# Second layer of a two-layer decoder: Gram masks, a pair's norm, key transposes and exponentials issued at other places

## The chip, the cores and the metric

The kernel runs on one core of one Trainium2 chip, as one program. The metric is the device time of one execution in microseconds; the median of three runs is compared. Five engines work beside each other, each through a queue of its own in the order that was fixed when the program was built: TensorE (PE in the profile; PEld is its loading of weights), VectorE (DVE), ScalarE (ACT), GpSimd (POOL) and SyncE (SP), which issues most of the transfers. An instruction that waits holds everything behind it in its queue.

## The reference, cut to what matters

Two residual layers work on 512 tokens of width 2048, in float32. The first is gated differential attention and isn't touched. The second is RWKV-7 time mixing with 32 heads of 64 channels:

```python
p = h @ w_in
p = p + (token_shift(p) - p) * mu
r, k, v, g, dw, da = jnp.split(p, RW_SPLITS, axis=-1)
w_log = -jax.nn.softplus(-(w0 + jnp.tanh(dw) @ decay_up)) - 0.5
decay = jnp.exp(-jnp.exp(w_log))
a = jax.nn.sigmoid(a0 + da @ iclr_up)
kk = heads(k * k_k)
kk = kk / jnp.maximum(jnp.sqrt(jnp.sum(kk * kk, axis=-1, keepdims=True)), 1e-12)
k = k * (1.0 + (a - 1.0) * k_a)
# wkv7_scan(r, decay, k, v, -kk, kk * a), for each token:
sa = jnp.einsum('bhvk,bhk->bhv', S, a_t)
S = S * w_t[:, :, None, :] + sa[..., None] * b_t[:, :, None, :] + v_t[..., None] * k_t[:, :, None, :]
y = jnp.einsum('bhvk,bhk->bhv', S, r_t)
# then
y = (y - mean) * lax.rsqrt(var + GN_EPS)
y = y * gn_w + gn_b + jnp.sum(r * k * r_k, axis=-1, keepdims=True) * v
x = x + (y * jax.nn.silu(g)) @ w_out
```

## The kernel before, in words

**Pairs.** The second layer goes through 16 pairs of heads (`j` from 0 to 15; 128 channels each). The 512 tokens lie in 8 chunks of 64. For a pair, four projections of the width 128 are computed one after the other: V of pair `j` (`proj(2, j)`), K of pair `j+1` (`begin(j + 1)`), the gate of pair `j-3` (from `j` = 3 on; `proj(3, j - LAG)`) and the receptance of pair `j+1` (`receptances(j + 1)`). Each is 48 matmuls of 128x512 (L129, into `pp`): 16 blocks of the contraction by three products of high and low parts, because float32 values are split in two parts. The weights of a projection are loaded in two halves, and for each half ACT makes two tiles of high parts (`wh`, L115) and DVE two of low parts (`wl`, L116).

**Positions.** Every projection matmul is a tick. What follows calls V18 the place behind the 18th matmul of V, and so K, g (gate) and r (receptance). `behind=[(at, f)]` calls `f` behind the matmul `at`. Two trains of small work advance on ticks: the scan of pair `j-1` (class `Chain`, `scan_pair`) and the triangular solve of pair `j` (class `Solve`, `t_solve`).

**The scan.** In a full pair (`j` from 3 to 14) it starts at V3, and the gaps between its steps are 7, 7 and 8 ticks. A chunk c has three steps: the matmul L1322 and the copy of its result to `rhs` (ACT, L1325); the matmul L1333 and the copy to `VS` (ACT, L1335); the matmul L1340 and the state for the next chunk, `VS` from DVE (L1344; L1347 for chunk 0). So L1322 of chunk c is at tick 3 + 22c, L1340 at 17 + 22c: L1340 of chunk 1 at V39, of chunk 4 at tick 105 of the pair (g9), of chunk 5 at 127 (g31), of chunk 6 at 149 (r5). POOL copies the state to `SA` (L1328) and scales it (`Sg`, L1331). `others` is work that goes behind the state of a given chunk: `turn_keys` (four transposes into the PSUM tag `pb`, L1171, and the copy to `BKT`, L1172) at chunks 0 and 1, that is at V17 and V39, `turn_values` at 4, `finish_y` at 5. After chunk 7 come `outputs` (L1362, L1366) and `centre` (`yc`, L1377 to L1379).

**The Gram matrices.** `gram` stands at V18: 32 matmuls (L1123), the first half into the two buffers of `pb`, the second into those of `pc`; ACT copies them to `G` (L1127) and to `LP` (L1132). Behind that, `mask_gram` sets triangles of `G` to zero on POOL (L1158, L1160; four instructions for a pair). The masked parts are read by the next pair's scan and its outputs. Then `t_solve`: 12 ticks on, at V30, the transpose `LT` (DVE, L1189), the bound and the reciprocal of the squared norms `n2` (L1195, L1196), then 31 steps of two DVE instructions (L1200, L1203), 3 or 4 ticks apart; they end at tick 138 of a full pair (g42), and there follow the product with `n2` (L1205) and the transposes `T1` (L1207) and `W` (L1210). `t_first` (L1230; r9) and `t_second` (L1245; r33) join the halves of the inverse.

**The norms.** `norms` (r24) sums the squares of the keys by two matmuls (L1043, L1044; `pt<-sHx,ones` and `pt<-sLx,ones`), copies them to `ssl` (L1144), and sends them through DRAM with three transfers from POOL's queue (L1148 twice, L1151) to lie as `n2`.

**Keys of the next pair.** `stage1` leaves three parts in `g.later`: `decays` (a scan on DVE, L1073, then the exponentials on ACT, L1077 to L1079, and `f`, L1080), `queries` (DVE, then the scales of `BK` on ACT, L1087) and `keys` (DVE product L1091, squares L1093, their split L916 and L917). One of them is traced behind each new state, so in a full pair behind chunks 4, 5 and 6. What is left over is traced at the head of `norms` or of `stage2`.

**The group norm** of a pair (`group_norm`: square `ysq` on ACT, L1387; sums L1389; an inverse root of eleven small DVE instructions, L63 to L70; the product L1393) is called at V18 of the pair after next.

**What sets the order.** The program is traced first, and a planner then gives each engine its order: of what is ready by its own reckoning it takes what has the highest priority. A priority falls with the place in the trace, `high_priority(offset)` raises it (scan 5000, solve 4000, weight splits 2000). So work that is ready early can be issued far ahead of its place. `issue_after(ins)` puts what a block traces behind `ins` on the same engine's queue; `behind(g, ins)` (the function, L1175) puts an instruction of any engine behind the matmul of the current tick, as an order for the planner with no wait at run time. Tiles of a tag share its buffers: `thg` has one buffer for the gate's `th`, `k2`, `ssl` and `ysq`, and a tile waits until the one before has been read.

Of the kernel before, what the change touches and what calls it, by code (L numbers as in the profile page):

```python
# [18 lines left out]
ALU = mybir.AluOpType  # L19
# [4 lines left out]
P = 128  # L24
D = 2048
# [927 lines left out]
C = 64  # L953
NC_ = T // C
HALF = 32
NG = 4
# [71 lines left out]
LAG = 3  # L1028
# [15 lines left out]
    g.nc.tensor.matmul(out, ones, l[:], start=False, stop=True)  # L1044


def stage1(g, j, k, up):


    nc, w = g.nc, g.work  # L1050
    p = Pair()
    col = lambda n: g.prm[n][:, j : j + 1]
    ch = lambda ap: ap.rearrange("p (c t) -> p c t", c=NC_)
    th = []
    for i, nm in enumerate(("hw0", "ha0")):
        (uH, uL), (xH, xL) = up, g.dwda[i]
        ps = g.ps.tile([P, 512], F32, name="pt", tag="pb", bufs=2)
        mm3(nc, ps[:], uH[:, i, :], uL[:, i, :], xH[:], xL[:], True, True)
        o = w.tile([P, T], F32, name=f"th{i}", tag=f"th{i}", bufs=1)
        nc.scalar.activation(o[:], ps[:], AF.Tanh, bias=col(nm), scale=0.5)  # L1060
        th.append(o)
    lw, tha = th
    nc.scalar.activation(lw[:], lw[:], AF.Identity, bias=g.hdec[:], scale=-0.5 * DECAY)
    l = w.tile([P, NC_, C], F32, name="l", tag="l", bufs=1)
    m = g.small.tile([P, NC_], F32, name="m", tag="m")
    p.E = w.tile([P, NC_, C + 1], F32, name="E", tag="E", bufs=1)
    p.gam = g.small.tile([P, NC_], F32, name="gam", tag="gam")
    p.AR = w.tile([P, NC_, 2, C], F32, name="AR", tag="AR", bufs=3)
    p.BK = w.tile([P, NC_, 2, C], F32, name="BK", tag="BK", bufs=1)
    p.f = w.tile([P, T], F32, name="f", tag="f", bufs=1)  # L1070

    def decays():
        nc.vector.tensor_tensor_scan(l[:].rearrange("p c t -> p (c t)"), g.rmask[:].rearrange("p c t -> p (c t)"),  # L1073
                                     lw[:], 0.0, ALU.mult, ALU.add)
        nc.vector.tensor_scalar(m[:], l[:, :, C - 1], 0.5, None, ALU.mult)
        nc.vector.tensor_sub(l[:], l[:], m[:, :, None].to_broadcast([P, NC_, C]))
        nc.scalar.activation(p.E[:, :, 0], m[:], AF.Exp, scale=-1.0)  # L1077
        nc.scalar.activation(p.E[:, :, 1:], l[:], AF.Exp)
        nc.scalar.activation(l[:], l[:], AF.Exp, scale=-1.0)  # L1079
        nc.scalar.activation(p.f[:], tha[:], AF.Identity, bias=col("omka"), scale=col("hka"))  # L1080

    def queries():
        nc.vector.tensor_mul(p.f[:], p.f[:], k[:])
        nc.vector.scalar_tensor_tensor(p.AR[:, :, 0, :], ch(k[:]), col("nkk"), p.E[:, :, 0:C], ALU.mult, ALU.mult)
        nc.vector.tensor_mul(l[:], ch(k[:]), l[:])
        for i in range(2):
            nc.scalar.activation(p.BK[:, :, i, :], ch(tha[:]), AF.Identity, bias=col(f"bk_b{i}"),  # L1087
                                 scale=col(f"bk_s{i}"))

    def keys():  # L1090
        nc.vector.tensor_mul(p.BK[:], p.BK[:], l[:, :, None, :].to_broadcast([P, NC_, 2, C]))  # L1091
        k2 = w.tile([P, T], F32, name="k2", tag="thg", bufs=1)
        nc.scalar.activation(k2[:], k[:], AF.Square, scale=col("kk"))  # L1093
        p.k2 = split_act(g, k2[:], w, "x")
        nc.vector.tensor_add(p.gam[:, 0 : NC_ - 1], m[:, 0 : NC_ - 1], m[:, 1:NC_])
        nc.scalar.activation(p.gam[:, 0 : NC_ - 1], p.gam[:, 0 : NC_ - 1], AF.Exp)

    g.later += [decays, queries, keys]
    return p

# [74 lines left out]
def behind(g, ins):  # L1175

    if g.at:
        g.tc.add_manual_dep(ins.ins, g.at.ins.name, mybir.DependencyInfo(mybir.DependencyClass.NoSync,
                            mybir.DependencyReason.DATA), reason="pace")


def t_solve(g, j, p):


    nc, w = g.nc, g.work
    NQ = HALF // NG
    yield 12
    LT = w.tile([P, HALF, HALF], F32, name="LT", tag="LT", bufs=1)
    nc.vector.transpose(LT[:].rearrange("p (r c) t -> p t r c", r=NG),  # L1189
                        p.LP[:].rearrange("p c t -> p t c")[:, :, None, :].to_broadcast([P, HALF, NG, NC_]))  # L1190
    Tm = w.tile([P, NQ, HALF], F32, name="Tm", tag="Tm", bufs=1)
    tmp = w.tile([P, NQ * HALF], F32, name="tmpl", tag="tmpl", bufs=1)
    nc.gpsimd.tensor_copy(Tm[:], g.unit[:])
    n2 = p.n2
    nc.vector.tensor_scalar(n2[:], n2[:], 1e-24, None, ALU.max)  # L1195
    nc.vector.reciprocal(n2[:], n2[:])  # L1196
    for i in range(HALF - 1):
        n, s = HALF - 1 - i, i // NG + 1
        tt = tmp[:, : n * s].rearrange("p (a b) -> p a b", a=s)
        st = nc.vector.scalar_tensor_tensor(tt, LT[:, i : i + 1, i + 1 :].to_broadcast([P, s, n]), n2[:, i : i + 1],  # L1200
                                       Tm[:, 0:s, i : i + 1].to_broadcast([P, s, n]), ALU.mult, ALU.mult)
        behind(g, st)
        nc.vector.tensor_add(Tm[:, 0:s, i + 1 :], Tm[:, 0:s, i + 1 :], tt)  # L1203
        yield 3 + i % 2
    nc.vector.tensor_mul(Tm[:], Tm[:], n2[:, None, :].to_broadcast([P, NQ, HALF]))  # L1205
    p.T1 = w.tile([P, NC_, HALF], F32, name="T1", tag="T1", bufs=1)
    nc.vector.transpose(p.T1[:].rearrange("p c (q r) -> p q r c", r=NG),  # L1207
                        Tm[:].rearrange("p q (r c) -> p q r c", r=NG))
    p.W = w.tile([P, NC_, HALF], F32, name="W", tag="Tm", bufs=1)
    nc.vector.transpose(p.W[:], p.T1[:])  # L1210
    for h in range(2):
        for half in range(2):
            o = half * HALF
            q = slice(h * C + o, h * C + o + HALF)
            nc.gpsimd.tensor_copy(g.TT[j % 2][q, :, h, o : o + HALF], p.W[q])
# [95 lines left out]
def scan_pair(g, j, p, gap, gap_s, others):  # L1311
# [3 lines left out]
    nc, w, VS = g.nc, g.work, p.VS  # L1315
# [4 lines left out]
    for c in range(NC_):  # L1320
# [1 line left out]
        nc.tensor.matmul(sm[:, 0:P], both(p.G[:, c, 0]), both(VS[:, c]), start=True, stop=True)  # L1322
        rhs = w.tile([P, C], F32, name="rhs", tag="rhs", bufs=2)
        for h, r_ in HEADS:
            nc.scalar.copy(rhs[r_, :], sm[r_, h * C : h * C + C])  # L1325
        if c:
            for h, r_ in HEADS:
                nc.gpsimd.tensor_copy(p.SA[r_, c - 1, :], VS[r_, c, h, :])  # L1328
# [76 lines left out]
def layer1(g, aps):  # L1405
    nc, tc = g.nc, g.tc
    with ExitStack() as cx:
# [18 lines left out]
        def receptances(j):  # L1426
            def piece(f, i, p):
                def follow(m):
                    with tc.high_priority(offset=SCAN), tc.issue_after(m.ins):
                        f(g, i, p)  # L1430
                return follow

            behind = [(24, lambda m: norms(g, j, pairs[j], m))]
            if j:
                behind += [(9, piece(t_first, j - 1, pairs[j - 1])), (33, piece(t_second, j - 1, pairs[j - 1]))]
            return shift_mix(g, proj(0, j, behind=behind), P, *mus(g, 0, j), "r", 1)

        begin(0)
# [1 line left out]
        for j in range(D // P):  # L1440
            p = pairs[j]
            if j:
                others = [(0, lambda p=p: turn_keys(g, p, 0)), (1, lambda p=p: turn_keys(g, p, 4)),
                          (4, lambda p=p: turn_values(g, p))]
                if j > 1:
                    others.append((5, lambda i=j - 2: finish_y(g, i, pairs[i])))
                full = LAG <= j < D // P - 1
                gaps = (7, 8) if full else (5, 6) if j < LAG else (4, 5)
                chain(g, j - 1, pairs[j - 1], 3, *gaps, others)
            stage2(g, j, r, p)  # L1450

            def behind(m, j=j, p=p):
                if j > 1:
                    pairs[j - 2].chain.finish(g)
                with tc.issue_after(m.ins):
                    gram(g, j, p)
                mask_gram(g, p, 0)
                mask_gram(g, p, 1)
                p.solve = Solve(g, t_solve(g, j, p))
                if j > 1:  # L1460
                    group_norm(g, j - 2, pairs[j - 2])

            stage_v(g, j, p, proj(2, j, behind=[(18, behind)]))
            if j == 0:
                turn_keys(g, p, 0)
                turn_keys(g, p, 4)
                turn_values(g, p)
            if j + 1 < D // P:
                begin(j + 1)
            if j >= LAG:  # L1470
                gated(g, j - LAG, pairs[j - LAG], gate(g, j - LAG, proj(3, j - LAG)))
            if j + 1 < D // P:
                r = receptances(j + 1)
        chain(g, j, p, 66, 5, 6, whole=True)
        gated(g, j - 2, pairs[j - 2], gate(g, j - 2, proj(3, j - 2)))
        gps = proj(3, j - 1)
# [75 lines left out]
def body(ctx, tc, nc, aps):  # L1552
    g = Ctx()
    g.nc, g.tc = nc, tc
    g.last, g.first = None, []
    g.chains, g.later, g.state, g.solve = [], [], None, None
    g.const = ctx.enter_context(tc.tile_pool(name="const", bufs=1))
    g.hp = ctx.enter_context(tc.tile_pool(name="hp", bufs=16))
    g.wraw = ctx.enter_context(tc.tile_pool(name="wrawp", bufs=3))
# [35 lines left out]
```

## Time and profile before

| what | value |
|---|---|
| median of three runs | 2182.38 us (2180.26 to 2183.14) |
| the profiled execution | 2186.34 us |
| its span, first to last instruction | 2184.6 us |
| mean granted TensorE clock | 0.998 |
| DVE, ACT and POOL busy | 70%, 51% and 15% of the span |
| first and last start of a Gram matmul (L1123) | 1040.6 us and 1939.5 us |

A busy time counts an instruction from its start to its end. Matmuls overlap: one of 128x512 takes 0.39 us, and the next starts 0.23 us after it, so a busy PE may still stand for a moment between two starts. Idle time in brackets in a timeline is that before the row, with what ended it. In the chain of waits each row is a piece of time and what it is put down to.

### The profile page before, as it was taken

To read this page: it belongs to the slowest core of one execution; us is meant where nothing else is said; L and a number is where in the kernel's file an instruction comes from. 1 tells how busy PE (TensorE), PEld (TensorE's weight loads), DVE (VectorE), ACT (ScalarE), POOL (GpSimd) and SP (SyncE) were. 2 spreads that over 40 slices of the span, in tenths; PEclk is the share of its full clock that TensorE was granted. 3 is DMA by queue.
4 is the path that set the end of the run, shared out by engine and by line. 5 is a ranking of instruction groups with operands and counts; after the bars stand their busy time and mean duration, and the time that the engine had idled before them with its cause. 6 is when DMAs were issued, how large, how long until landed. Compare 5 with 4: busy or idle time off the path is not lost.

```text
span 2184.6 us, 34849 instructions
## 1 busy us (share of the span) xinstructions
PE 2147.5 (98%) x12260; PEld 1756.3 (80%) x12260; DVE 1524.7 (70%) x4137; ACT 1120.4 (51%) x2523; POOL 328.0 (15%) x614
## 2 busy tenths in 40 slices
PE   9999999999999999999999999999999999999999
PEld 8888888888888878878777877877778787777887
DVE  5665646465665667466788888878888888887645
ACT  6443434344443454345666656565666565655333
POOL 0000000000000000120233222222222222332001
PEclk9999999999999999999999999999999999999999
DMA  6323232222223356562222222222222223345565
GB/s 194 96 80 97 87 97 92 92 89 87 95 87 97 115 184 221 155 136 80 73 65 67 76 76 68 77 74 76 76 76 76 75 62 83 83 125 183 174 168 122
DMA packets 258623, 225.76 MB, mean 103 GB/s; under 512 B 12336, under 2 KB 220480, under 8 KB 258448
## 3 DMA queue, kind: packets, MB, share of 16 engines
q1 hardware_dynamic: 239504, 188.03, 28.9%
q0 software_dynamic: 10080, 19.50, 4.5%
q10 hardware_dynamic: 8864, 16.01, 2.0%
q8 instruction: 96, 1.57, 0.3%
q14 instruction: 79, 0.65, 0.1%
HBM read 207.50 MB, written 15.99 MB: 102 GB/s over the span
## 4 chain that ended last, share of the span: by engine, by line
PE 79%; ACT 8%; DVE 8%; issue 3%; DMA 1%; ACTq 0%; POOL 0%; DVEq 0%; POOLq 0%
PE pp L129 61%; PE pt L129 5%; ACT wh L115 1%; DVE wl L116 1%; PE o L129 1%; PE sc L129 1%; DVE LT L1189 1%; PE sm L1340 1%; PE sm L1322 1%; ACT G L1127 1%; PE lora L129 1%; PE gp L1123 1%; DVE VS L1344 1%; PE sm L1333 1%; DVE l L1073 1%
## 5 line engine op out<-in xcount | busy, mean ns | idle before, releaser
L116 DVE TENSOR_TENSOR wl<-wraw,wh 128x512 fp32r<-128x512 f32 (+1 forms) x636 | 447.2, 705 | 411.0 <-ACT wh L115 404.5
L115 ACT CAST wh<-wraw 128x512 fp32r<-128x512 f32 (+1 forms) x636 | 392.8, 619 | 535.6 <-PE pp L129 432.2
L129 PE MATMUL pp<-wh,hH 128*128 128x512 f32 x1268 | 500.2, 394 | 0.8 <-DVE prmin_rw_mu_dram L234 0.6
L129 PE MATMUL pp<-wh,hL 128*128 128x512 f32 x1268 | 497.6, 393 | 0.0
L129 PE MATMUL pp<-wl,hH 128*128 128x512 f32 x1268 | 497.2, 392 | 0.0
L129 PE MATMUL pp<-hH,wh 128*128 128x512 f32 x1024 | 416.7, 407 | 0.0
L129 PE MATMUL pp<-hL,wh 128*128 128x512 f32 x1024 | 414.4, 405 | 0.0
L129 PE MATMUL pp<-hH,wl 128*128 128x512 f32 x1024 | 413.5, 404 | 0.0
L129 PEld LDWEIGHTS pp<-wh,hH 128*128 128x128 f32 x1268 | 238.3, 188 | 49.0 <-issue 1.3
L129 PEld LDWEIGHTS pp<-wh,hL 128*128 128x128 f32 x1268 | 238.2, 188 | 48.8 <-DVE hL L908 0.3
L129 PEld LDWEIGHTS pp<-wl,hH 128*128 128x128 f32 x1268 | 238.3, 188 | 46.9
L129 PEld LDWEIGHTS pp<-hH,wh 128*128 128x128 f32 x1024 | 193.5, 189 | 35.9
L129 PEld LDWEIGHTS pp<-hH,wl 128*128 128x128 f32 x1024 | 194.0, 189 | 32.9
L129 PEld LDWEIGHTS pp<-hL,wh 128*128 128x128 f32 x1024 | 193.6, 189 | 32.0
L1200 DVE SCALAR_TENSOR_TENSOR tmpl<-LT,n,Tm 128x60 f32<-128x60 f32 (+24 forms) x496 | 135.2, 272 | 13.2
L1328 POOL COPY SA<-VS 64x64 f32<-64x64 f32 x224 | 74.2, 331 | 430.7 <-DVE VS L1344 354.0
L500 POOL DMA_DIRECT2D frow<-yd x12 | 8.9, 742 | 803.5 <-DVE rs_t L67 675.9
L1203 DVE TENSOR_TENSOR Tm<-Tm,tmpl 128x60 f32<-128x60 f32 (+24 forms) x496 | 104.7, 211 | 12.5
L1325 ACT COPY rhs<-sm 64x64 f32<-64x64 f32 x256 | 52.6, 205 | 75.8 <-PE sm L1322 73.3
L1335 ACT COPY VS<-sm 64x64 f32<-64x64 f32 x256 | 52.8, 206 | 68.2 <-PE sm L1333 64.0
L1322 PEld LDWEIGHTS sm<-VS,G 128*128 128x128 f32 x256 | 46.0, 189 | 32.7 <-issue 14.1
L1344 DVE SCALAR_TENSOR_TENSOR VS<-sm,gam,Sg 64x64 f32<-64x64 f32 x192 | 53.8, 280 | 24.9 <-PE sm L1340 20.5
(339 smaller groups left out, 3259.8 us busy)
## 6 DMA issues: line engine op xcount, KB each, us to landing
wraw<-in_rw_w_in_dram SPq DMA_DIRECT2D x128, 512.0 KB, 4.0
wraw<-in_da_w_in_dram SPq DMA_DIRECT2D x254, 256.0 KB, 3.0
wraw<-in_da_w_out_dram SPq DMA_DIRECT2D x26, 512.0 KB, 4.5
wraw<-in_rw_w_out_dram SPq DMA_DIRECT2D x26, 512.0 KB, 4.2
yr<-yd SPq DMA_DIRECT2D x28, 256.0 KB, 3.6
frow<-yd POOLq DMA_DIRECT2D x12, 512.0 KB, 6.5
xq<-in_x_dram SPq DMA_DIRECT2D x16, 256.0 KB, 5.2
xd<-xq ACTq DMA_DIRECT2D x16, 256.0 KB, 3.9
```

The source lines that it names most:

```text
L115: nc.scalar.copy(hi[:], raw[:, k : k + n])
L116: nc.vector.tensor_sub(lo[:], raw[:, k : k + n], hi[:].bitcast(F32))
L129: m = nc.tensor.matmul(out, a, b, start=s, stop=e, skip_group_check=skip)
L1073: nc.vector.tensor_tensor_scan(l[:].rearrange("p c t -> p (c t)"), g.rmask[:].rearrange("p c t -> p (c t)"), lw[:], 0.0, ALU.mult, ALU.add)
L1123: m = nc.tensor.matmul(gp[h][:, i * P : (i + 1) * P], BK[r_, c0 + i, :, :], p.AR[r_, c0 + i, :, :], start=True, stop=True)
L1200: st = nc.vector.scalar_tensor_tensor(tt, LT[:, i : i + 1, i + 1 :].to_broadcast([P, s, n]), n2[:, i : i + 1], Tm[:, 0:s, i : i + 1].to_br ...
L1203: nc.vector.tensor_add(Tm[:, 0:s, i + 1 :], Tm[:, 0:s, i + 1 :], tt)
L1322: nc.tensor.matmul(sm[:, 0:P], both(p.G[:, c, 0]), both(VS[:, c]), start=True, stop=True)
L1325: nc.scalar.copy(rhs[r_, :], sm[r_, h * C : h * C + C])
L1328: nc.gpsimd.tensor_copy(p.SA[r_, c - 1, :], VS[r_, c, h, :])
L1335: nc.scalar.copy(VS[r_, c, h, :], sm[r_, P : P + C])
L1344: g.state = nc.vector.scalar_tensor_tensor(VS[r_, c + 1, h, :], s_, p.gam[r_, c : c + 1], Sg[r_, :], ALU.mult, ALU.add)
```

## The change

The change edits the second layer alone; no arithmetic is added or left out.

- `turn_keys` goes from chunks 0 and 1 to chunks 1 and 2 of the scan (V39 and K13).
- The exponentials of `decays` with `f`, and the scales of `queries`, are put into a list `g.soon`, and traced behind the copy to `rhs` of the next chunk with the scan's priority (or ahead of `queries` and `keys`, if none came).
- `mask_gram` goes from V18 to r6 of the next receptance; for the last pair it stays.
- `norms` goes from r24 to r39, `t_first` from r9 to r12.
- In `t_solve` the transpose `LT` is put behind the matmul of its tick, and the bound and reciprocal of `n2` behind `LT`; `T1` comes 9 ticks later and `W` 4 more, each behind its tick's matmul.
- `group_norm` of pair `j-1` is called behind the receptance of `j+1`, where it was called at V18 of the next round.
- The scan in the round of `j` = 1 starts at tick 22 with gaps of 4, 4 and 5, where it started at 3 with 5, 5 and 6.

```diff
+def soon(g):
+    while g.soon:
+        g.soon.pop(0)()
...
         nc.vector.tensor_sub(l[:], l[:], m[:, :, None].to_broadcast([P, NC_, C]))
+        g.soon.append(exponentials)
+
+    def exponentials():
         nc.scalar.activation(p.E[:, :, 0], m[:], AF.Exp, scale=-1.0)
         nc.scalar.activation(p.E[:, :, 1:], l[:], AF.Exp)
         nc.scalar.activation(l[:], l[:], AF.Exp, scale=-1.0)
         nc.scalar.activation(p.f[:], tha[:], AF.Identity, bias=col("omka"), scale=col("hka"))
 
     def queries():
+        soon(g)
...
         nc.vector.tensor_mul(l[:], ch(k[:]), l[:])
+        g.soon.append(scales)
+
+    def scales():
         for i in range(2):
             nc.scalar.activation(p.BK[:, :, i, :], ch(tha[:]), AF.Identity, bias=col(f"bk_b{i}"),
                                  scale=col(f"bk_s{i}"))
 
     def keys():
+        soon(g)
...
-    nc.vector.transpose(LT[:].rearrange("p (r c) t -> p t r c", r=NG),
+    lt = nc.vector.transpose(LT[:].rearrange("p (r c) t -> p t r c", r=NG),
...
-    nc.vector.tensor_scalar(n2[:], n2[:], 1e-24, None, ALU.max)
-    nc.vector.reciprocal(n2[:], n2[:])
+    behind(g, lt)
+    with g.tc.issue_after(lt.ins):
+        nc.vector.tensor_scalar(n2[:], n2[:], 1e-24, None, ALU.max)
+        nc.vector.reciprocal(n2[:], n2[:])
...
-    nc.vector.transpose(p.T1[:].rearrange("p c (q r) -> p q r c", r=NG),
+    yield 9
+    tt = nc.vector.transpose(p.T1[:].rearrange("p c (q r) -> p q r c", r=NG),
                         Tm[:].rearrange("p q (r c) -> p q r c", r=NG))
     p.W = w.tile([P, NC_, HALF], F32, name="W", tag="Tm", bufs=1)
-    nc.vector.transpose(p.W[:], p.T1[:])
+    behind(g, tt)
+    yield 4
+    tt = nc.vector.transpose(p.W[:], p.T1[:])
+    behind(g, tt)
...
         for h, r_ in HEADS:
-            nc.scalar.copy(rhs[r_, :], sm[r_, h * C : h * C + C])
+            rc = nc.scalar.copy(rhs[r_, :], sm[r_, h * C : h * C + C])
+        with g.tc.issue_after(rc.ins):
+            soon(g)
...
-            behind = [(24, lambda m: norms(g, j, pairs[j], m))]
+            behind = [(39, lambda m: norms(g, j, pairs[j], m))]
             if j:
-                behind += [(9, piece(t_first, j - 1, pairs[j - 1])), (33, piece(t_second, j - 1, pairs[j - 1]))]
+                behind += [(6, lambda m: [mask_gram(g, pairs[j - 1], h) for h in range(2)]),
+                           (12, piece(t_first, j - 1, pairs[j - 1])), (33, piece(t_second, j - 1, pairs[j - 1]))]
...
-                others = [(0, lambda p=p: turn_keys(g, p, 0)), (1, lambda p=p: turn_keys(g, p, 4)),
+                others = [(1, lambda p=p: turn_keys(g, p, 0)), (2, lambda p=p: turn_keys(g, p, 4)),
...
-                gaps = (7, 8) if full else (5, 6) if j < LAG else (4, 5)
-                chain(g, j - 1, pairs[j - 1], 3, *gaps, others)
+                gaps = (7, 8) if full else (5, 6) if j == 2 else (4, 5)
+                chain(g, j - 1, pairs[j - 1], 3 if j > 1 else 22, *gaps, others)
...
-                mask_gram(g, p, 0)
-                mask_gram(g, p, 1)
+                if j + 1 == D // P:
+                    mask_gram(g, p, 0)
+                    mask_gram(g, p, 1)
                 p.solve = Solve(g, t_solve(g, j, p))
-                if j > 1:
-                    group_norm(g, j - 2, pairs[j - 2])
...
                 r = receptances(j + 1)
+                if j:
+                    group_norm(g, j - 1, pairs[j - 1])
```

More of the change, by code (lines that the diff above doesn't have):

```diff
@@ L1555, in body @@
     g.last, g.first = None, []
-    g.chains, g.later, g.state, g.solve = [], [], None, None
+    g.chains, g.later, g.soon, g.state, g.solve = [], [], [], None, None
     g.const = ctx.enter_context(tc.tile_pool(name="const", bufs=1))
```

## The prediction

> **What bounds the kernel now.** The page first, for the engine that sets the time; then its busy time by stretches, cut from the first Gram matmul of a pair to that of the next.
>
> ```profile
> PE 2147.5 (98%) x12260; PEld 1756.3 (80%) x12260; DVE 1524.7 (70%) x4137; ACT 1120.4 (51%) x2523; POOL 328.0 (15%) x614
> ```
>
> ```profile
> 1313.40:1375.20 61.80, 60.76 (x421) 49.13 (x420) 50.61 (x140) 37.48 (x91) 17.35 (x35) 1.00 0.28 76
> 1437.00:1501.60 64.60, 62.18 (x421) 50.41 (x420) 53.27 (x141) 37.60 (x91) 17.09 (x34) 0.97 0.26 72
> 1687.20:1752.20 65.00, 62.08 (x421) 50.33 (x421) 53.77 (x144) 37.65 (x91) 16.96 (x35) 0.97 0.26 72
> ```
>
> The columns are the length, the busy time and count of PE, PEld, DVE, ACT and POOL, the granted clock, the DMA share and GB/s. TensorE bounds everything, and the change takes no matmul from it, so a gain can only be time in which it stands. A full pair takes 61.8 us; two take 64.6 and 65.0 with the same 421 matmuls, at a lower clock. So I looked for what TensorE waits for, in the whole run, and in one ordinary pair by the chain of waits.
>
> ```profile
> PE sm L1322 <- DVE VS L1344: 13.9, 16, 2.4
> PE sm L1340 <- ACT VS L1335: 3.2, 14, 0.3
> PE pt L1043 <- ACT sHx L916: 2.8, 14, 0.2
> ...
> PE sm L1333 <- ACT rhs L1325: 1.1, 2, 0.8
> ```
>
> ```profile
> 1318.34 1.53 DVE wl L116
> 1319.88 2.16 DVE LT L1189
> ...
> 1324.08 0.30 DVE VS L1344
> ...
> 1324.52 0.46 PE sm L1322 x2
> ...
> 1345.28 0.63 ACT E L1078
> 1345.93 0.20 ACT rhs L1325
> ...
> 1346.38 0.52 ACT l L1079
> ...
> 1348.25 0.20 ACT VS L1335
> ...
> 1349.67 1.85 PE pp L129 x8
> ...
> 1363.08 0.63 ACT sHx L916
> 1363.75 0.40 PE pt L1043
> ```
>
> The first view gives total, times and longest. Three places come back in each pair: the scan's state behind the transpose `LT` on VectorE (1324.52), a chunk's `rhs` and `VS` behind exponentials on ScalarE (1345.93 to 1348.25), and the norms' matmul behind the split of the squares (1363.75). These waits are understated where a matmul's 0.39 us covers the next start, so I size two places by starts on TensorE.
>
> ```profile
> 1313.44 2.56 PE L1123 MATMUL gp<-AR,BK 64*128 64x128 f32 x32
> ...
> 1341.84 0.38 PE L1340 MATMUL sm<-VS,BKT 128*128 128x128 f32 x2
> ...
> 1348.74 0.38 PE L1340 MATMUL sm<-VS,BKT 128*128 128x128 f32 x1 [0.22 <-ACT VS L1335]
> ...
> 1355.05 0.27 PE L1340 MATMUL sm<-VS,BKT 128*128 128x128 f32 x1
> ...
> 1937.69 2.06 PE L1123 MATMUL gp<-AR,BK 64*128 64x128 f32 x32
> ```
>
> **The change part by part.** *Key transposes a chunk on.* In a full pair they stand at V17, just ahead of the Gram matmuls, and take one of the two buffers of `pb` that the first Gram half needs; the 32 matmuls take 2.56 us. In the last pair, whose scan has other gaps and no transposes there, they take 2.06. Behind the change V17 is free: 12 full pairs x 0.50 = 6.0 us. The transposes' own time only moves, to K13; V39 has four of them before and after.
>
> *Exponentials and scales behind `rhs`.* From L1340 of chunk 4 to that of chunk 5 it is 1348.74 - 1341.84 = 6.90 us, from chunk 5 to chunk 6 1355.05 - 1348.74 = 6.31, with the same 22 projection matmuls, three scan steps and four transposes. The first stretch loses 0.59. With `rhs` ahead of the exponentials (0.63 and 0.52 for the two large ones) ScalarE does them while TensorE runs the seven matmuls to the next step (0.23 each, from the eight in 1.85 us, so 1.6): 12 x 0.59 = 7.1 us. If they overrun with `f`, `VS` is late as it is now (0.22). Bounds 0 and 7.1; I take 7.1, since 1.15 fits into 1.6.
>
> *Norms at r39.* The split of the squares ends at 1363.71, and 15 ticks are 3.5 us, so the 14 waits of 2.8 us go. What the norms issue moves by the same 3.5 us, with its three transfers on POOL's queue:
>
> ```profile
> 1366.57 0.39 POOL L1193 CAST Tm<-unit 128x256 f32<-128x256 bf16 x1 [0.17 <-PE px L1245]
> ...
> 1369.73 0.57 POOL L1151 DMA_DIRECT2D n<-nd  x1 [2.07 <-DMA nd<-ssl]
> ```
>
> The last transfer was issued at 1369.73; it becomes about 1373.2. `n2` lands later by as much, too late for its old place on VectorE, but that place moves behind `LT`, which a period later starts at 1319.9 + 61.8 = 1381.7. In a long pair it was late already:
>
> ```profile
> 1436.73 0.18 DVE L1195 TENSOR_SCALAR n<-n 128x32 f32<-128x32 f32 x1 [0.97 <-DMA n<-nd]
> ...
> 1437.45 0.35 DVE L1196 RECIPROCAL n<-n 128x32 f32<-128x32 f32 x1
> ...
> 1441.69 1.61 DVE L1393 TENSOR_TENSOR yc<-yc,rsg 128x512 f32<-128x512 f32 x1
> ```
>
> ```profile
> 1449.45 0.35 PE L1322 MATMUL sm<-VS,G 128*128 128x128 f32 x1 [1.89 <-DVE VS L1344]
> ...
> 1451.13 0.63 PE L129 MATMUL pp<-hH,wl 128*128 128x512 f32 x1
> ```
>
> ```profile
> 1147.69 0.46 PE L1322 MATMUL sm<-VS,G 128*128 128x128 f32 x2 [1.43 <-DVE VS L1344]
> ...
> 1148.68 0.40 PE L129 MATMUL pp<-hH,wl 128*128 128x512 f32 x1
> ```
>
> *The two long pairs.* Here `n2` came 0.97 us late and held VectorE's queue; the group norm behind it ran into the masks on POOL, `LT` came late, and TensorE stood 1.89 us. Behind that wait a matmul takes 0.63 us for 0.39: the clock fell. Behind the 1.43 of another pair a matmul still takes 0.40. With L1195 behind `LT` and the group norm gone from there, this chain loses its first two links: 64.6 + 65.0 - 2 x 61.8 = 6.0 us. [...]
>
> *Masks.* They run beside VectorE's work:
>
> ```profile
> 1316.63 1.58 POOL L1158 TENSOR_SCALAR_AFFINE_SELECT G<-G 64x512 f32<-64x512 f32 x2 [1.67 <-ACT G L1127]
> ...
> 1318.18 2.72 POOL L1160 TENSOR_SCALAR_AFFINE_SELECT G<-G 64x1024 f32<-64x1024 f32 x2
> ```
>
> In 1316.6 to 1320.9 an L116 that else takes 0.69 us (row of 1367.88 below) takes 1.53. In the receptance they would meet the transposes, L1344 of chunk 6 and L1091 instead. But a place in the trace does not hold POOL back: L1193, traced at V30, was issued at 1366.57, in r34. The masks are ready at 1316.6 in either version, and nothing ties them to r6, so I expect them where they were and cost the edit at nothing; bounds in the rivals.
>
> *The wait behind `LT`.* The product that held `LT` back stays if the masks stay. Behind `LT` now come L1195 and L1196 (0.18 + 0.35), so the state is 0.5 us later unless the planner, with `LT` held to V30, puts it ahead of the second step or of L116 (0.69). Without the three waits shown (2.4, 1.9 and 1.4) it is (13.9 - 5.7) / 13 = 0.6 us in a pair. It may go (-8.2 in all) or grow by 0.5 in 12 pairs (+6). I take nothing, near the middle.
>
> *Group norm in the receptance.*
>
> ```profile
> 1367.22 0.62 ACT L115 CAST wh<-wraw 128x512 fp32r<-128x512 f32 x1
> 1369.85 0.62 ACT L115 CAST wh<-wraw 128x512 fp32r<-128x512 f32 x1 [2.01 <-PE pp L129]
> ...
> 1371.09 0.62 ACT L1387 ACTIVATE ysq<-yc 128x512 f32<-128x512 f32 x1
> ```
>
> ```profile
> 1365.20 0.76 DVE L1379 TENSOR_TENSOR yc<-Y,s 128x256 f32<-128x256 f32 x2
> 1367.88 0.69 DVE L116 TENSOR_TENSOR wl<-wraw,wh 128x512 fp32r<-128x512 f32 x1 [1.92 <-ACT wh L115]
> ```
>
> `yc` is there at 1366.0, and both engines then stand for 2 us at a time; the square waits for `thg`, which `ssl` holds until its transfers are read (1369.73). With `ssl` at r39 the square can come first, and the norm's work on VectorE goes into that idle time. No time of its own on the path; it is the cover of the two terms above.
>
> *The rest.* `T1` moves from about r0 to r3, 9 ticks (2.1 us) ahead of `t_first` and takes under 0.7; the scan in the round of `j` = 1 no longer crosses its Gram matmuls, which ends that pair's longest wait for `rhs` (0.8): about 1 us. For new small waits from twelve moved pieces I give back 2 us, an estimate.
>
> Sum: 6.0 + 7.1 + 2.8 + 6.0 + 1.0 - 2.0 = 20.9 us. The profiled execution took 2186.3, so 2165.4; the median of the runs shown lies 4.0 below that execution, which gives 2161.5.
>
> **The rivals.** *The state gets later.* The two instructions behind `LT` add their 0.5 us to the wait in 12 pairs: 6 of 20.9 go, 2167.5. For it: the rows 1319.88 to 1324.08, VectorE has no gap there. Against it: it need not come in that order.
>
> *The masks do move*, and meet the solve's end. VectorE is held by up to 4.3 us of POOL in each receptance, `W`, L1344 and L1091 slip, `t_first` or chunk 7 wait by about the 0.84 us (1.53 - 0.69) that one product lost: 12 x 0.84 = 10, less 4 for a quicker `LT` or not: 2167 to 2172. [...] Against it: nothing holds the masks there.
>
> *Slower.* The square `ysq` is issued behind `ssl`. Then it waits for the buffer until transfers that are 3.5 us later have been read, about 1373.2, and the group norm runs under the masks in every full pair as it did in two. It decides from where the wait of TensorE passes 1.43 towards 1.89 us and the clock falls. Each of ten more pairs then loses 3.0 us and the two gain none: 30 - (20.9 - 6.0) = 15 us more, 2197. For it: one buffer, four users. Against it: 2 us of idle ScalarE just ahead of r39.
>
> *It does little.* The planner finds another order with as much waiting, since it plans without these delays: 2178 to 2187.
>
> **How the numbers follow.** Chances: forecast with its own range (2150 to 2167) 0.60, later state 0.13, moved masks 0.09, little 0.05, slower 0.13. The low end is the sum with the wait behind `LT` gone, nothing given back (-8.2 - 2.0), and about 1 us for starts that the waits understate: 2182.4 - 32 = 2150. The high end takes in the first two rivals and part of the third: 2179. A measurement here tells about 0.2%, 4.4 us, from no change. Faster by more is the first three cases, 0.82; same 0.05; slower 0.13.
>
> **What would show it.** Gram matmuls of 2.06 us in full pairs; equal L1340 distances (6.3) for chunks 5 and 6; no wait of L1043; all full pairs alike, without a clock of 0.97; `ysq` ahead of `ssl`; L1195 right behind `LT` with no wait for its transfer. The forecast is wrong if pairs stay at 61.8 or above, if a wait for L1344 over 1.8 us shows in ordinary pairs, or if POOL's masks lie in the receptance.

## The result

| kernel | median, us | range, us | runs |
|---|---|---|---|
| before | 2182.61 | 2180.26 to 2183.56 | 7 |
| changed | 2189.51 | 2188.26 to 2192.64 | 7 |

The changed kernel takes 1.0033 times the time of before, with a 95% interval of 1.0022 to 1.0045: slower by 0.3%, where 2161.5 us had been forecast. The profiled execution has a span of 2188.4 us at a mean clock of 0.996. One execution in the experiments below, of the kernel with `n2` back where it was, took 2849 us at a granted clock of 0.687 and is left out of that kernel's median and range.

TensorE's waits in the changed kernel come first (total, times, longest; the step L1322 is now L1341, the state L1344 is L1365):

```profile
PE sm L1341 <- DVE VS L1365: 30.2, 17, 2.6
...
PE sm L1361 <- ACT VS L1356: 0.7, 2, 0.4
PE sm L1354 <- ACT rhs L1344: 0.6, 2, 0.3
```

The waits behind the exponentials (L1340, 3.2 us before) and for the squares (L1043, 2.8) are gone from the list or nearly so. One row grew, the scan's state behind `LT`, from 13.9 to 30.2 us. Two pairs by stretches (length, then busy time and count of PE, PEld, DVE, ACT and POOL, clock, DMA share, GB/s):

```profile
1315.22:1378.65 63.43, 61.15 (x423) 50.15 (x422) 53.47 (x140) 37.23 (x91) 17.41 (x34) 0.97 0.28 73
1378.65:1440.75 62.10, 59.78 (x423) 48.86 (x422) 53.23 (x140) 37.22 (x91) 17.42 (x34) 1.00 0.28 75
```

An ordinary full pair takes 62.1 us where it took 61.8. Four of the twelve are longer, at 63.4 to 63.75, with a lower clock. The timeline of all engines in the pair from 1315.22 on shows the link that is late:

```profile
1314.69 0.63 ACT L1408 ACTIVATE ysq<-yc 128x512 f32<-128x512 f32 x1
1315.22 2.06 PE L1136 MATMUL gp<-AR,BK 64*128 64x128 f32 x32
...
1316.13 0.69 DVE L1410 TENSOR_REDUCE var<-ysq 128x8 f32<-128x512 f32 x1
...
1318.11 1.43 POOL L1171 TENSOR_SCALAR_AFFINE_SELECT G<-G 64x512 f32<-64x512 f32 x2 [1.10 <-ACT G L1140]
...
1319.05 0.50 DVE L67 TENSOR_TENSOR rs_t<-rs_i 128x8 f32<-128x8 f32 x1
...
1319.50 2.40 POOL L1173 TENSOR_SCALAR_AFFINE_SELECT G<-G 64x1024 f32<-64x1024 f32 x2
...
1319.59 1.09 DVE L68 SCALAR_TENSOR_TENSOR rs_t<-rs_t,var 128x8 f32<-128x8 f32 x1
...
1320.71 0.17 DVE L70 SCALAR_TENSOR_TENSOR rsg<-rs_t,rs_i 128x8 f32<-128x8 f32 x1
...
1320.91 1.53 DVE L1414 TENSOR_TENSOR yc<-yc,rsg 128x512 f32<-128x512 f32 x1
...
1322.97 2.18 DVE L1202 STREAM_TRANSPOSE LT<-LP 128x1024 f32<-128x1024 f32 x1
...
1325.06 0.13 DVE L1210 TENSOR_SCALAR n<-n 128x32 f32<-128x32 f32 x1
...
1326.81 0.60 DVE L1365 SCALAR_TENSOR_TENSOR VS<-sm,gam,Sg 64x64 f32<-64x64 f32 x2
...
1327.55 0.46 PE L1341 MATMUL sm<-VS,G 128*128 128x128 f32 x2 [2.28 <-DVE VS L1365]
```

The norms' transfers are now issued 5.9 us ahead of the Gram matmuls, by POOL's rows:

```profile
1309.30 1.17 POOL L1161 DMA_DIRECT2D nd<-ssl  x2 [2.41 <-ACT ssl L1157]
```

They read `ssl`, and the square `ysq`, which takes its buffer, starts only 0.53 us ahead of the Gram matmuls, where it stood 4.1 us ahead of them before. (The last transfer from POOL, which waits for those that read `ssl`, is issued at 1312.34; from there to 1314.69 `ysq` stands behind three other instructions in ScalarE's queue.) So its root is worked out beside the masks on POOL. Of its nine small instructions of 128x8 in L67, L68 and L70, three take 0.50 to 1.09 us here and the others 0.17, and the product L1414 takes 1.53 where it takes 0.69 ahead of the masks. `LT` starts 7.75 us behind the first Gram matmul (6.4 before), and TensorE stands for 2.28. A wait of this length in ordinary pairs is one of the signs by which the prediction said that it would be wrong.

What the forecast expected of the rest is there too. The Gram matmuls take 2.06 us in a full pair, and `n2` (1325.06) follows `LT` without a wait. L1361 of chunks 4, 5 and 6 stands at equal distances of 6.18:

```profile
1346.71 0.38 PE L1361 MATMUL sm<-VS,BKT 128*128 128x128 f32 x2
1352.89 0.38 PE L1361 MATMUL sm<-VS,BKT 128*128 128x128 f32 x2
1359.07 0.38 PE L1361 MATMUL sm<-VS,BKT 128*128 128x128 f32 x2
```

### The profile page after: what moved, and what is told of

Its sections match the earlier page's. It is cut to its first block, busy times and chain, and to the rows that moved or that the text cites. A ratio compares the mean times of both kernels' runs of the same rounds, so it can differ in the third digit from the quotient of the medians.

```text
span 2188.4 us, 34852 instructions
## 1 busy us (share of the span) xinstructions
PE 2138.8 (98%) x12260; PEld 1755.7 (80%) x12260; DVE 1555.2 (71%) x4137; ACT 1118.5 (51%) x2523; POOL 328.2 (15%) x614
## 4 chain that ended last, share of the span: by engine, by line
PE 83%; DVE 11%; ACT 2%; issue 2%; DMA 1%; POOL 0%; DVEq 0%; ACTq 0%; POOLq 0%
PE pp L129 65%; PE pt L129 5%; DVE wl L116 2%; DVE LT L1202 2%; PE sm L1341 1%; PE o L129 1%; PE sc L129 1%; DVE rs_t L68 1%; PE lora L129 1%; PE sm L1354 1%; PE sm L1361 1%; PE Y L1383 1%; DMA yr<-yd 1%; ACT wh L115 1%; PE pt L346 1%
## 5 line engine op out<-in xcount | busy, mean ns | idle before, releaser
L116 DVE TENSOR_TENSOR wl<-wraw,wh 128x512 fp32r<-128x512 f32 (+1 forms) x636 | 441.9, 697 | 399.0 <-ACT wh L115 386.3
L1349 POOL COPY SA<-VS 64x64 f32<-64x64 f32 x224 | 68.9, 307 | 510.5 <-DVE VS L1365 451.4
L1344 ACT COPY rhs<-sm 64x64 f32<-64x64 f32 x256 | 53.1, 207 | 85.5 <-PE sm L1341 83.5
L1341 PEld LDWEIGHTS sm<-VS,G 128*128 128x128 f32 x256 | 45.9, 188 | 50.4 <-issue 34.4
L1341 PE MATMUL sm<-VS,G 128*128 128x128 f32 x256 | 51.2, 282 | 31.7 <-DVE VS L1365 30.2
```

The source lines that it names most:

```text
L116: nc.vector.tensor_sub(lo[:], raw[:, k : k + n], hi[:].bitcast(F32))
L1344: rc = nc.scalar.copy(rhs[r_, :], sm[r_, h * C : h * C + C])
```

## The experiments

The theory: the only fault is that `ysq` shares its one buffer with `ssl`, which the norms at r39 hold for 3.5 us longer; everything else in the change pays about as forecast. The rivals: the two instructions of `n2` behind `LT` delay the state; or the masks do. Each ratio is against the kernel before on the same chip. A "full pair" is the time from first Gram matmul to first Gram matmul, and the excess is what lies over 0.23 us between the start of L1341 of chunk 2 and that of the matmul ahead of it, worked out from the starts in the trace: 0.71 in an ordinary pair of before, 2.44 in the changed kernel.

**Norms back at r24** (the rest of the change kept).

```diff
-            behind = [(39, lambda m: norms(g, j, pairs[j], m))]
+            behind = [(24, lambda m: norms(g, j, pairs[j], m))]
```

> The changed kernel with the norms back at r24, all else kept. Theory A (the group norm is late: its square shares the one buffer of thg with ssl, ssl is 4 us later at r39, so the norm's small VectorE work falls under POOL's masks and holds LT): the norm is back where it was, the wait of L1341 behind the state falls from 2.44 us to between 0.3 and 0.9 us in full pairs, no clock drop, the norms' wait of 0.2 us returns; about 2165 us. Theory B (the wait comes from the bound and reciprocal of n2 put behind LT and from what the planner puts between LT and the state): the wait stays above 2 us, about 2188. Theory C (the masks alone, whenever they run beside VectorE): they stay at V18, so about 2188.

Measured: 2159.18 us (2158.68 to 2160.05), ratio 0.9891 (0.9877 to 0.9906). Waits and two pairs:

```profile
PE sm L1341 <- DVE VS L1365: 7.5, 16, 0.8
```

```profile
1309.73:1369.79 60.06, 59.64 (x423) 48.99 (x422) 51.07 (x140) 37.29 (x90) 18.15 (x34) 1.00 0.29 78
1369.79:1429.83 60.04, 59.63 (x423) 48.98 (x422) 51.05 (x140) 37.28 (x90) 18.14 (x34) 1.00 0.29 78
```

One number in the change decides between 0.3% slower and 1.1% faster. And of the 14 waits that the move was to end one alone comes back, with 0.2 us. ScalarE's and TensorE's rows of an ordinary pair:

```profile
1357.38 0.62 ACT L916 CAST sHx<-k 128x512 fp32r<-128x512 f32 x1
...
1358.74 0.40 PE L1043 MATMUL pt<-sHx,ones 128*2 128x512 f32 x1
```

With the other edits the split ends at 1358.00, 0.7 us ahead of the norms' matmul at r24. So the move bought nothing here.

**`ysq` in another buffer** (norms at r39; in the loop it uses the tag `l`).

```diff
-    sq = w.tile([P, NG, C], F32, name="ysq", tag="thg", bufs=1)
+    sq = w.tile([P, NG, C], F32, name="ysq", tag=tag, bufs=1)
...
-                    group_norm(g, j - 1, pairs[j - 1])
+                    group_norm(g, j - 1, pairs[j - 1], "l")
```

> The changed kernel with the square of the group norm in the buffer of tag l, which is free from r10 on, inside the loop over the pairs. Norms stay at r39, masks at V18. Theory A: the norm's work goes into the receptance ahead of V; the wait of L1341 falls to 0.3 to 0.9 us, about 2160 us. Theory B: wait above 2 us, about 2188. Theory C: the masks still run beside L116 and the end of LP's copies, so the wait stays above 1.5 us, about 2180.

Measured: 2162.31 us (2161.90 to 2164.12), ratio 0.9907 (0.9892 to 0.9922).

```profile
1301.88 0.63 ACT L1408 ACTIVATE ysq<-yc 128x512 f32<-128x512 f32 x1 [2.42 <-DVE yc L1400]
...
1306.16 0.17 DVE L70 SCALAR_TENSOR_TENSOR rsg<-rs_t,rs_i 128x8 f32<-128x8 f32 x1
```

The square now waits for `yc` alone and stands 9.1 us ahead of the Gram matmuls (1310.95); the root is done 4.6 us ahead of them, with 0.17 for each small instruction. So it was the buffer, and not the priority or ScalarE, that put `ysq` behind `ssl`. Full pairs take 60.2, the excess is 0.58. Only the first full pair is still late (62.3).

**Masks held at r6**, by an order of the planner behind the tick's matmul (`ms` are a head's two masks; with the shared buffer, and then with `ysq` in `l`).

```diff
+        for x in ms:
+            behind(g, x)
...
-                behind += [(6, lambda m: [mask_gram(g, pairs[j - 1], h) for h in range(2)]),
+                behind += [(6, lambda m: [mask_gram(g, pairs[j - 1], h, m) for h in range(2)]),
```

> The changed kernel with the masks held to r6 by an order for the planner behind the matmul of r6 (the change's words, made true). The norm stays late. Theory A: the norm is late but no longer held by POOL (the four stretched instructions take 3.6 us for 1.2), so LT starts when its input is there, 2 us earlier; wait 0.3 to 0.9 us, about 2165, less what the masks cost in the receptance (bound: 0.8 us in 12 pairs, 10 us). Theory B: wait above 2 us, 2188. Theory C: like A.

> Both: square in the buffer of tag l, and masks held to r6. Theory A: little more than the better of the two alone, since LT waits for its input LP in each of them: 2156 to 2163, unless the masks now meet the norm or the solve's end in the receptance. Theory B: 2188. Theory C: same as the run with the masks held alone.

Measured: 2172.14 us (2171.63 to 2172.93), ratio 0.9951 (0.9936 to 0.9965), and 2172.27, ratio 0.9951 (0.9935 to 0.9968). The waits of the first (the state is L1369, T1 is L1227):

```profile
PE sm L1345 <- DVE VS L1369: 13.5, 29, 0.9
PE px L1253 <- DVE T L1227: 2.7, 11, 0.8
```

Without masks beside it, the late group norm does no harm: the excess at chunk 2 is 0.49 with `ysq` as late as before (0.53 us ahead of the Gram matmuls), and the second kernel, with `ysq` early, takes the same time (it had been expected at 2156 to 2163). So the loss needs both, a late norm and the masks there. But held in the receptance the masks make two other waits in each pair, one at chunk 7 and one for `T1`. VectorE shows them there (the products of the steps before and behind this one take 0.23):

```profile
1290.02 1.12 DVE L1219 SCALAR_TENSOR_TENSOR tmpl<-LT,n,Tm 128x16 f32<-128x16 f32 x1
```

Full pairs take 61.1, against 60.2 with `ysq` early and the masks where they were: 0.9 each, near the 0.84 of the rival on the masks.

**Parts alone, on the kernel before.** The norms at r39; the key transposes at chunks 1 and 2; the exponentials and scales behind `rhs`.

```diff
+            behind = [(39, lambda m: norms(g, j, pairs[j], m))]
...
+                others = [(1, lambda p=p: turn_keys(g, p, 0)), (2, lambda p=p: turn_keys(g, p, 4)),
...
+        with g.tc.issue_after(rc.ins):
+            soon(g)
```

> The kernel before with one edit: the norms at r39 for r24. Theory A (group norm late behind ssl) says that this one edit makes the loss: the square is issued some 3 to 4 us later, the norm falls under the masks, and the two small n2 instructions, still ahead of it in VectorE's queue, wait for their transfer as well; wait of L1322 behind the state 2 us or more in each full pair, with clock drops: 2200 to 2225 us. Theory B (n2 behind LT is the cause, and it isn't in this kernel): 2180 to 2183, less the norms' wait of 2.8.

> The kernel before with one edit: key transposes at chunks 1 and 2. By the prediction's first term the Gram matmuls of the 12 full pairs fall from 2.56 to 2.06 us: 6.0 us less, about 2177. If the stretch behind the Gram matmuls only gets shorter for TensorE, but LP's copies and LT do not come sooner, half a microsecond a pair comes back as a longer wait behind LT: 2183.

> The kernel before with the exponentials and the scales behind the copies to rhs, and nothing else. By the prediction's second term the distance of L1340 from chunk 4 to chunk 5 falls from 6.9 to 6.3 us in 12 pairs: 7.1 us less, about 2176. If f and the scales hold the copies to VS instead, the distance stays above 6.6 and the time at 2180 or more.

Measured: 2189.15 us (2187.41 to 2191.15), ratio 1.0033 (1.0021 to 1.0046); 2177.75 (2173.42 to 2182.03), 0.9983 (0.9974 to 0.9993); 2169.98 (2168.90 to 2172.18), 0.9949 (0.9934 to 0.9964).

The norms at r39 alone lose what the whole change loses, though not in the same way, and less than the 2200 to 2225 that had been expected (in most pairs the excess at chunk 2 is 0.97 and not 2): most pairs lose 0.1 us (61.93), the round ahead of the first full pair 2.3 (53.9 for 51.7), and two full pairs are long, as in the profiled execution of before. `ysq` stands 0.96 us ahead of the Gram matmuls, and the masks start 3.19 us behind the first of these, where in the changed kernel they start at 2.89, so the root meets only the first of them (one L68 of 0.57 us).

```profile
1319.07:1381.00 61.93, 60.77 (x421) 49.21 (x420) 51.67 (x140) 37.34 (x91) 17.00 (x34) 1.00 0.28 75
1381.00:1445.41 64.41, 62.21 (x421) 50.49 (x420) 52.85 (x140) 37.42 (x91) 16.56 (x34) 0.97 0.27 72
```

The keys alone make ordinary full pairs 0.8 us shorter (61.0), but three are long, two of them with `n2` held for 0.56 and 0.43 us by its transfer. The Gram matmuls' 0.5 is in these 0.8. The exponentials alone make them 0.85 shorter (60.97): 0.72 from chunk 4 to 5 and 0.13 from 5 to 6. No pair is long in their profiled execution.

```profile
1339.20 0.38 PE L1355 MATMUL sm<-VS,BKT 128*128 128x128 f32 x2
1345.39 0.38 PE L1355 MATMUL sm<-VS,BKT 128*128 128x128 f32 x2
1351.57 0.38 PE L1355 MATMUL sm<-VS,BKT 128*128 128x128 f32 x2
```

**`n2` back where it was** (norms at r24, the rest of the change kept).

```diff
-    with g.tc.issue_after(lt.ins):
-        nc.vector.tensor_scalar(n2[:], n2[:], 1e-24, None, ALU.max)
-        nc.vector.reciprocal(n2[:], n2[:])
+    nc.vector.tensor_scalar(n2[:], n2[:], 1e-24, None, ALU.max)
+    nc.vector.reciprocal(n2[:], n2[:])
```

> The changed kernel with the norms at r24, and the bound and reciprocal of n2 put back where they stood (not behind LT). By the forecast the two instructions leave the place behind LT and the state comes up to 0.53 earlier in ordinary pairs, but a late transfer of the norms holds VectorE's queue again in one to three pairs, with 2 us of wait and 1 us of clock each where it does: 2159.2 - 12 x 0.3 + 2 x 3.0 = 2162. If the late transfers of the kernel before came from its exponentials or its key transposes instead, no pair is long and the time is 2154 to 2157.

Measured: 2180.0 us (2171.4 to 2184.6), ratio 0.9992 (0.9979 to 1.0005). The forecast's mechanism, but some 21 us over the run with the norms at r24 alone, where 3 had been expected: the profiled execution has four long pairs of 62.9 to 64.3, and the others run longer than it.

```profile
1309.00 0.18 DVE L1208 TENSOR_SCALAR n<-n 128x32 f32<-128x32 f32 x1 [1.60 <-DMA n<-nd]
...
1315.51 1.01 DVE L70 SCALAR_TENSOR_TENSOR rsg<-rs_t,rs_i 128x8 f32<-128x8 f32 x1
```

```profile
1322.37 0.63 PE L1340 MATMUL sm<-VS,G 128*128 128x128 f32 x2 [3.29 <-DVE VS L1364]
```

The transfer's landing differs from pair to pair. Where it is 1.6 us late, in two of the long pairs (0.55 and 0.94 in the other two), the root runs under the masks as in the changed kernel, and TensorE stands for 3.29 in the pair shown. An ordinary pair is 0.2 us shorter than with `n2` behind `LT` (59.85 for 60.04), but the edit is worth 1% of the time against this.

**The state ahead of the solve's first step**, in all rounds (norms at r24).

```diff
         nc.vector.reciprocal(n2[:], n2[:])
+    yield 10
...
-    yield 9
+    yield 1
...
-    yield 4
+    yield 2
```

> The run with the norms at r24 (2159 us), and in the solve the 31 steps begin 10 ticks behind LT; T1 then 1 tick and W 2 ticks on. The planner puts the state of chunk 1 ahead of the first step and of L116. If what is left of the wait of L1341 (0.5 to 0.9 us) is these instructions, it falls to 0.2 or less: 2152 to 2155. If it is LT itself, which starts when LP is there, 2158 or more; if T1 now comes late for t_first, a wait of L1249 shows.

Measured: 2168.45 us (2165.76 to 2168.71), ratio 0.9938 (0.9923 to 0.9953). The wait behind `LT` went in the full pairs, but two early stretches became longer (54.1 for 50.8 and 67.5 for 60.4), and `px` waited for `T1` in full ones:

```profile
1189.50:1257.00 67.50, 65.27 (x466) 52.93 (x460) 51.55 (x143) 41.93 (x101) 18.94 (x39) 0.95 0.29 77
1257.00:1317.30 60.30, 59.54 (x423) 48.87 (x422) 49.96 (x140) 37.51 (x90) 17.39 (x34) 1.00 0.29 77
```

The early rounds have no gate, so 48 ticks fewer, and the later start of the solve pushes its end into the next pair's Gram matmuls, which take 5.5 to 8.0 us there in place of 2.06.

**The same in full pairs alone**, with the first 20 steps 3 ticks apart so that `T1` and `W` keep their ticks (with norms at r24, and with r39 and `ysq` in `l`).

```diff
+    full = LAG <= j < D // P - 1
+    if full:
+        yield 10
...
-        yield 3 + i % 2
+        yield 3 if full and i < 20 else 3 + i % 2
```

> The changed kernel with the norms at r24 (2159.2), and in full pairs alone the first step of the solve comes 10 ticks after the norms' reciprocal (behind V40), with the first 20 steps 3 ticks apart instead of 3 and 4, so that T1 and W keep their ticks; the rounds of j below 3 and the last keep theirs. If the wait behind LT is what these two instructions and a step cost, the start of L1341 of chunk 2 loses nothing more (it lost 0.53 in most pairs, 0.96 in some), full pairs take 59.5, and the time is 2159.2 - 12 x 0.53 = 2153, with no clock fall. If the loss of 9 us in the run with the yields in all rounds belonged to the full pairs (T1 late for px), it shows here again: 60.3 for a full pair, 2162 or more.

> The changed kernel with the square in the buffer of tag l (2162.3, norms at r39), and the same edit of the solve in full pairs. There the wait of a full pair is 0.58. If it goes, 2162.3 - 12 x 0.58 = 2155.3, and periods of 59.65. The difference to the run beside it then says what the norms' place is worth once the square doesn't wait for them: by the forecast 2.4 us in favour of r39 (12 waits of 0.2), by the two runs before it 3 us in favour of r24.

Measured: 2147.45 us (2145.64 to 2148.79), ratio 0.9847 (0.9832 to 0.9861), and 2150.29 (2148.54 to 2151.75), ratio 0.9860 (0.9843 to 0.9876). The first is the fastest of all, 1.5% below the kernel before and 10 to 12 us below the run with the norms at r24 alone (by the ratios and by the medians, which come from two chips). Both are some 5 us better than expected, of which the chips may make 2 to 3: their medians of the kernel before are 2183.45 and 2180.85. Beside each other the two runs say that r24 is the better place by 2.8 us even where the square doesn't wait for the norms; it is 3.1 without this edit.

```profile
1426.10:1485.26 59.16, 59.16 (x421) 49.05 (x420) 50.93 (x140) 37.20 (x90) 18.21 (x34) 1.00 0.29 79
```

```profile
1433.96 0.17 DVE L1210 TENSOR_SCALAR n<-n 128x32 f32<-128x32 f32 x1
1434.17 0.35 DVE L1211 RECIPROCAL n<-n 128x32 f32<-128x32 f32 x1
1434.44 0.63 DVE L116 TENSOR_TENSOR wl<-wraw,wh 128x512 fp32r<-128x512 f32 x1
1435.10 0.60 DVE L1368 SCALAR_TENSOR_TENSOR VS<-sm,gam,Sg 64x64 f32<-64x64 f32 x2
```

A full pair takes 59.16, 0.9 less than before this edit. The excess of 0.53 at chunk 2 is gone in most pairs. With the first step of the solve out of the way, the state follows `n2` and one L116. The next chunk gains as well: from L1361 of chunk 2 to that of chunk 3 it was 6.46 with the norms at r24 alone and is 6.18.

## Why the prediction was wrong, by its steps

**The step that failed** is the one on the group norm in the receptance: "With `ssl` at r39 the square can come first, and the norm's work on VectorE goes into that idle time." It can't. A tile of a one-buffer tag gets the buffer in the order of the trace, `norms` is traced in the receptance and `group_norm` behind it, so `ysq` comes behind `ssl` and its transfers however idle ScalarE is. With its own buffer `ysq` moved from 0.53 to 9.1 us ahead of the Gram matmuls, and the time went to 2162.31. That is within 1 us of the 2161.5 of the forecast, which had assumed such a place. That it is so close is luck in part: other terms were off both ways, as the paragraphs below say.

**The rival "Slower" named this mechanism** with a chance of 0.13, and put 2197 on it, 7.5 too much. It took the price of the long pairs of before, 3.0, for each. Measured, an ordinary pair loses 62.1 - 60.23 = 1.87 against the kernel with the other buffer, and four of them lose 1.3 to 1.65 beyond that, mostly as the clock falls (to a granted 0.50, for 3.41 us in each). The first full pair is as long in both (62.3), and the rounds ahead of it lose 2.8 together: 11 x 1.87 + 4 x 1.46 + 2.8 = 29. The profiled executions differ by 28.2, the medians by 27.2. The chance was too small: the arguments for it (one buffer, four users) were facts of the program, that against it (2 us of idle ScalarE) only room.

**Terms that held.** *Gram matmuls*: 2.06 in full pairs as forecast; the key transposes alone made ordinary full pairs 0.8 shorter, not 0.50. *Masks*: they stayed behind the copies of `G` (1318.11), as argued from L1193; holding them at r6 costs the 10 us of the rival. *The two long pairs*: the chain was as described, with `n2` the first link, but its price wasn't. `n2` behind `LT` was taken as worth 6.0, and is worth some 21 (2180.0 - 2159.2) with the rest of the change in place. For the kernel before much of the 6.0 was probably counted twice, since the sum also takes off 4.0 from the profiled execution to the median: with the exponentials alone no pair is long either, and that run's profiled execution is 17.2 us below the one of before, its median only 11.4.

**Terms with another size, cause or sign.** *Exponentials behind `rhs`*: 0.85 a pair, not 0.59, and 12 x 0.85 = 10.2 of the 11.1 us that the part alone gained (0.0051 x 2182). The stretch from chunk 5 to 6, used as the measure of one without loss, lost 0.13 itself. *Norms at r39*: the 2.8 us of waits went, but they go at r24 as well, since the other edits bring the split 0.7 us ahead of the matmul; against r24 the place at r39 costs 3 us where 2.8 were to be gained. *The wait behind `LT`*: 0.58 in place of 0.71 with `ysq` early, near the nothing that was taken. The row's bound of -8.2 was the more interesting end: with the first step later, full pairs gain 0.9 each.

## What to carry to other kernels

Before an instruction is counted into idle time, follow its tile: which tag, how many buffers, who holds it in the order of the trace and until which transfer is read. A step that moves a holder by some us moves everything that shares the buffer, and a chain off the critical path becomes the path where it runs into another engine's work: here the norm's root beside the masks on POOL, with 2.28 us in which TensorE stands. When a bundle of edits loses, take its edits back one at a time: here one number out of seven edits was the whole loss, and its gain came for nothing from the others.

## What the runs showed of the hardware

**In the changed kernel's trace the clock fell by a grid of 3.41 us, not by the length of one wait.** The stretches of the changed kernel, cut at the clock's own steps in the trace's clock records; the sixth row is a stretch of a pair with as long a wait, cut elsewhere, and the two in the second block cut that pair by the steps:

```profile
1325.50:1328.91 3.41, 1.36 (x7) 1.22 (x8) 2.99 (x12) 1.25 (x4) 0.95 (x3) 1.00 0.26 77
1328.91:1332.33 3.42, 3.42 (x11) 2.74 (x10) 3.25 (x10) 0.69 (x3) 0.00 (x0) 0.50 0.12 19
1332.33:1335.74 3.41, 3.41 (x19) 2.89 (x19) 3.13 (x12) 1.82 (x3) 1.23 (x3) 1.00 0.46 135
1513.23:1516.64 3.41, 1.48 (x8) 1.30 (x9) 3.01 (x12) 1.25 (x4) 0.95 (x3) 1.00 0.26 77
1516.64:1520.06 3.42, 3.42 (x11) 2.75 (x10) 3.28 (x10) 0.57 (x3) 0.00 (x0) 0.50 0.13 24
1388.00:1391.41 3.41, 1.12 (x7) 0.69 (x6) 3.08 (x10) 0.62 (x1) 0.66 (x3) 1.00 0.48 140
```

```profile
1386.94:1390.35 3.41, 1.74 (x8) 1.11 (x6) 3.19 (x7) 1.16 (x2) 0.00 (x0) 1.00 0.57 154
1390.35:1393.76 3.41, 2.79 (x14) 2.44 (x15) 3.03 (x13) 1.10 (x3) 0.95 (x3) 1.00 0.01 2
```

In these rows the granted clock goes from 1.00 to 0.50 for exactly one stretch behind one in which TensorE was busy for 1.36 or 1.48 of 3.41 us. In the full pairs the falls lie 187.73 us apart, which is 55 times 3.4133 (the fall at 1055.85 lies 273.06 us ahead of the one at 1328.91, 80 times 3.4133), and three pairs (62.1 + 62.1 + 63.5) take as long. So every third pair has its wait inside one stretch of the grid and pays; the wait at 1388, as long (2.29 us, where the one of the first row is 2.28), leaves TensorE busy for 1.12 in a stretch cut to hold it, but lies across two of the grid (1.74 and 2.79) and costs no clock. In this trace the forecast's threshold, between 1.43 and 1.89 us of wait, was therefore no threshold. A stretch that was idle for 2.05 of 3.41 us (the first row) or 1.93 (the fourth) was enough. From 1040 us on, every stretch of the grid in this trace that was idle for 1.93 us or more is followed by a fall, and none that was idle for up to 1.80. The nearest of these without a fall:

```profile
1574.67:1578.08 3.41, 1.61 (x8) 0.99 (x6) 3.19 (x7) 1.03 (x2) 0.00 (x0) 1.00 0.58 154
```

Idle time by these rows isn't the whole measure, though. In the run with the state first in all rounds the clock fell behind a stretch of 48 matmuls in which TensorE was busy for 2.60 of 3.42:

```profile
1136.48:1139.90 3.42, 2.60 (x48) 2.00 (x48) 3.06 (x11) 3.30 (x9) 1.34 (x4) 1.00 0.02 5
1139.90:1143.31 3.41, 3.34 (x15) 2.45 (x15) 0.57 (x2) 1.60 (x5) 1.53 (x4) 0.50 0.00 0
```

What counts in that stretch stays open.

**VectorE instructions of 128x8 took up to 1.09 us.** Beside the masks on POOL some of L67, L68 and L70 stretch to 0.50 to 1.09 us where 0.17 is usual. Ahead of the masks, in the run with `ysq` in `l`, all nine take 0.16 or 0.17 (1304.56 to 1306.16). In the full pairs of the changed kernel each stretched one ends within 0.02 us of the end of a mask; those that start within 0.02 us of the start of a mask keep 0.17. Here L67 ends at 1319.55 with the second of the two L1171 (1318.11 + 1.43 = 1319.54), and L68 at 1320.68 with the first L1173:

```profile
1319.50 1.16 POOL L1173 TENSOR_SCALAR_AFFINE_SELECT G<-G 64x1024 f32<-64x1024 f32 x1
```

So in these pairs a stretched instruction lasted until the end of POOL's, however small it was itself.
